# Expert weights in 32 KB homes, a scan of both halves in one tile, and x2 transposes with their squares in PSUM

## The chip, the cores and the metric

The kernel runs on one core of a Trainium2 chip. The core has a matrix engine (PE), a vector engine (DVE), a scalar engine (ACT), GpSimd (POOL) and the SP queue, which issues all loads and stores here; the data moves on 16 DMA engines. The metric is the time of one execution on the device in microseconds, as a median of several runs.

## What is computed

One layer of a decoder for 256 tokens of width 2048, in float32. The first half is a block of two mixers; the second is a mixture of 32 experts, of which each token uses two.

```python
h = rms_norm(x, attn_norm_g)
u_ssm, q, k, v, gate_ssm, gate_att = jnp.split(h @ w_in, splits, axis=-1)
y_ssm = s5_mixer(u_ssm, ...)      # 64 groups, 64 complex states each:
                                  # s[t] = abar * s[t-1] + bbar u[t];  y = Re(C s) + d u
                                  # z = gelu(y); y_ssm = z * sigmoid(z @ w_glu)
y_att = stick_breaking_attention(rms_norm(q), rms_norm(k), v)    # 8 heads of 128
merged = sigmoid(gate_ssm) * (y_ssm @ w_branch_ssm) + sigmoid(gate_att) * (y_att @ w_branch_att)
x = x + merged @ w_out
h2 = rms_norm(x, ffn_norm_g)
# router: top 1 of 4 groups, then top 2 of the 8 experts in it -> combine[t, e]
for e in range(32):               # w_gate, w_up: 2048 x 512; w_down: 512 x 2048
    hid = silu(h2 @ w_gate[e]) * (h2 @ w_up[e])
    out = out + combine[:, e:e + 1] * (hid @ w_down[e])
x = x + out
```

## The kernel before

**Dense stage.** All dense weights are streamed in 200 steps of 512 KB. In each step SP loads a tile `raw` five steps ahead (`dma`, L129), ACT casts it to `wh`, DVE makes the remainder `wl = raw - wh` two steps ahead (`split`), and PE runs 12 matmuls of 128x512. `raw`, `wh` and `wl` have three buffers each. The matrices follow each other as u, qkv, gates, branch weights `wba`, `wglu` (steps 144 to 151), `wbs` (152 to 167) and `wout` (168 to 199). Between the steps a planner runs generators for the small work: `init_stats`, `attention` with `heads`, `ssm`, `scan` and `gelu`. Each is resumed while the estimated loads of PE, DVE and ACT (the class `Meter`, through which every operation of the three engines goes, so that they all have line L77 in the profile) stay within a bound of one another; a negative yield makes a generator rest for some steps.

**Scan.** The states of the mixer lie in two tiles `Vs`, one for each half of the groups, [128, 2, 16, 128]. `scan` (L502 to L521) walks over the 127 last columns: for each column and half one product `prod` of 128x64 and two additions of 128x32, as soon as that half is ready. Then `ssm` makes `y` out of it block by block with matmuls against `CBD`.

**Residual and router.** After `wout`, `x2_tr(n, t)` (L380 to L394) transposes a quarter of row block t of `x2` into a PSUM tile `ps` (`bga`), ACT copies it out to `xt2`, and the sum of squares is taken by ACT (n < 3) or DVE (n = 3) with the squares themselves written to a spare tile `junk`. At the end of the dense stage DVE reduces the sums (`r2`), and a chain of small operations makes the router's choice. `gather(q)` then fetches the tokens of four experts into `XB`.

**Experts.** `gate_up` (L1109) uses four pieces of weights (k4 = 0 to 3, 32 matmuls of 128x256 each), `down` (L1137) two; after every fourth expert `scatter` adds the results. A piece is 2 MiB, [128, 4, 1024] float32, 16 KB for each partition, and in memory, too, each partition's 16 KB lie in one run. The pieces go through a ring of eleven 16 KB slots: eight units `U` that the dense stage has stopped using, and three slots that come when its pools are closed; from piece 22 on, ten slots. `load_piece` (L867 to L886) issues one load as soon as the next slot has been used. The first seven pieces are loaded under the dense stage as 28 single loads of 512 KB (L881), one in every second step from step 136 on, which stand in the list `ahead` and go out after the step's `raw` (L953); the eighth goes out near step 196. All loads stand in the one SP queue. At the end, `gate_up` of experts 30 and 31 runs `keep_busy(24)`, 24 transposes of a constant, ahead of each piece, and the down pieces come last, in the order 30, 31, 30, 31; the very last is loaded in two halves of 1 MiB.

Of the kernel before, what the change touches and what calls it, by code (L numbers as in the profile page):

```python
# [17 lines left out]
P = 128  # L18
T = 256
# [63 lines left out]
def hybrid_block(ctx, tc, A, out):  # L83
# [7 lines left out]
    U = {i: ctx.enter_context(tc.tile_pool(name=f"u{i}", bufs=1)) for i in range(11) if i != 6}  # L91

    def unit(i, shape, dt, name):
        return U[i].tile(shape, dt, name=name, tag="u")

    def slot(h, shape, dt, name):
        return hp.tile(shape, dt, name=name, tag=f"h{h}")
# [5 lines left out]
    hp = wctx.enter_context(tc.tile_pool(name="hp", bufs=1))  # L103
# [57 lines left out]
    uge = cq.tile([P, P], F32, name="uge")  # L161
# [5 lines left out]
    nmask = cq.tile([P, P], F32, name="nmask")  # L167
# [149 lines left out]
    def glu_fin(n):  # L317
        def f(a):
            if n == 0:
                ys = unit(7, [P, 2, 8, T], F32R, "ys")  # L320
# [59 lines left out]
    def x2_tr(n, t):  # L380
        ps = bg_tile(0)
        for i in range(4):
            k = 4 * n + i
            pe.transpose(ps[:, P * i:P * i + P], S["x2"][:, t, P * k:P * k + P], ident)
        xt = S["xt2"][n, t] = slot((2 * n + t) % 4, [P, 4, P], F32, "xt2")
        act.copy(xt, ps.rearrange("p (i c) -> p i c", i=4))
        junk = slot(4 + (2 * n + t) % 4, [P, 512], F32, "junk")
        xs = S["x2"][:, t, 512 * n:512 * n + 512]
        if n < 3:
            act.activation(junk, xs, AF.Square, accum_out=ssq[:, t, n:n + 1])  # L390
# [70 lines left out]
    xsq01 = slot(0, [P, 2, T], F32, "xsq01")  # L461
    xsq = [xsq01[:, 0], xsq01[:, 1], slot(1, [P, T], F32, "xsq2")]
# [36 lines left out]
    coef = [cq.tile([P, 2, 2, 16], F32, name=f"coef{h}") for h in range(2)]  # L499
    prod = [cq.tile([P, 2, 2, 16], F32, name=f"prod{h}") for h in range(2)]  # L500

    def scan(Vs):  # L502
        at = [1, 1]
        while ("V", 0) not in prog:
            yield 0
        yield -1
        while min(at) < P:
            on = [h for h in range(2) if ("V", h) in prog and at[h] < P]
            for h in on:
                X, c = Vs[h], at[h]  # L510
                vec.tensor_tensor(prod[h], X[:, :, :, c - 1][:, :, None, :].to_broadcast([P, 2, 2, 16]), coef[h], op=OP.mult)
            for k in range(2):
                for h in on:
                    X, c = Vs[h], at[h]
                    vec.tensor_tensor(X[:, :, :, c], X[:, :, :, c], prod[h][:, k], op=OP.add)
            for h in on:
                at[h] += 1
            if len(on) == 1:
                load["vec"] += 0.4
            yield 1 if on else 0  # L520
        prog["scan"] = True  # L521

    def ssm():
# [72 lines left out]
        for h in range(2):  # L596
            hs = slice(16 * h, 16 * h + 16)
            SE.tensor_copy(coef[h][:, 0, 0], a2r[:, hs])
            SE.tensor_copy(coef[h][:, 0, 1], a2i[:, hs])
            SE.tensor_scalar(coef[h][:, 1, 0], a2i[:, hs], -1.0, None, op0=OP.mult)  # L600
            SE.tensor_copy(coef[h][:, 1, 1], a2r[:, hs])
# [74 lines left out]
        CB = cq.tile([P, 16, 32], F32, name="CB")  # L676
# [17 lines left out]
        Vs = [unit(7 + h, [P, 2, 16, P], F32, f"Vs{h}") for h in range(2)]  # L694
        gens.append(scan(Vs))
        gens.append(gelu())
        for b in range(8):
            tiles = [bg_tile(0), bg_tile(1)]
            for ri in range(2):
                for i in range(2):  # L700
                    r = slice(64 * i, 64 * i + 64)
                    for a in range(2):
                        pe.matmul(tiles[i][:, T * a + P * ri:T * a + P * ri + P], BT[r, 2 * b + a, ri], uS[r, 2 * b + a],
                                  start=True, stop=True, tile_position=(64 * i, 0))
            for i in range(2):
                src = tiles[i].rearrange("p (a r c) -> p r a c", a=2, r=2)
                j = 4 * (b % 4) + i
                act.copy(Vs[b // 4][:, :, j:j + 3:2], src)
            if b % 4 == 3:
                prog["V", b // 4] = True  # L710
            yield 0
# [3 lines left out]
        for b in range(8):  # L715
            pp = [bg_tile(0), bg_tile(0)]
            X = Vs[b // 4]
            for par in (1, 0):
                ps = pp[par]
                for si in range(3):  # L720
                    for j in range(4):
# [6 lines left out]
                        elif par == 1:  # L728
                            pe.matmul(ps[js, 0:P], CBD[:, si - 1, 4 * b + j], X[:, si - 1, i],
                                      start=False, stop=(si == 2), tile_position=(0, 32 * j))  # L730
                        else:
                            pe.matmul(ps[js, 1:P], CBD[:, 1 + si, 4 * b + j], X[:, si - 1, i, 0:P - 1],
# [5 lines left out]
    def gelu():  # L738
# [4 lines left out]
        zz = unit(9, [P, 2, 8, T], F32R, "zz")  # L743
# [28 lines left out]
    def attention():  # L772
# [20 lines left out]
        QT = [slot(h, [P, 2, T], F32, f"qkT{h}") for h in range(8)]  # L793
# [11 lines left out]
        AT = unit(4, [P, 2, 2, 2, 3, P], F32, "AT")  # L805
        gens.insert(0, heads(QT, AT[:, 0], (0, 2)))
        gens.insert(1, heads(QT, AT[:, 1], (4, 6)))

    def heads(QT, at, firsts):
# [4 lines left out]
        for h0 in firsts:  # L814
# [32 lines left out]
            for i in range(2):  # L847
                y = slot(h0 + i, [P, 2, T], F32R, f"ya{h0 + i}")
# [7 lines left out]

    ring = [U[i] for i in (10, 8, 9, 2, 7, 4, 3, 1)]
    used = [0]
    held = {}
    ahead = []  # L860
    pieces = [(e, i) for e in range(NE - 2) for i in range(6)]
    pieces += [(e, i) for e in (NE - 2, NE - 1) for i in range(4)]
    pieces += [(e, i) for i in (4, 5) for e in (NE - 2, NE - 1)]
    ptile = {}
    nextp = [0]

    def load_piece():  # L867
        n = nextp[0]
        if n >= len(pieces):
            return  # L870
        j = n % 11 if n < 22 else (n - 22) % 10
        j += n >= 22 and j > 5
        if used[0] <= held.get(j, -1):
            return
        held[j] = n
        e, i = pieces[n]
        tl = ring[j].tile([P, 4, 1024], F32, name="ew", tag="u")
        src = A["wgu"][e][:, 4 * i:4 * i + 4] if i < 4 else A["wd"][e][:, 4 * i - 16:4 * i - 12]
        if n < 7:
            for k in range(4):  # L880
                ahead.append(lambda k=k: sp.dma_start(tl[:, k], src[:, k]))  # L881
        else:
            for c0, cw in (((0, 1024),) if n < len(pieces) - 1 else ((0, LSPLIT), (LSPLIT, 1024 - LSPLIT))):
                sp.dma_start(tl[:, :, c0:c0 + cw], src[:, :, c0:c0 + cw])
        ptile[e, i] = tl
        nextp[0] += 1  # L886

# [29 lines left out]
    first_out = nsub - 32  # L917
    for i in range(nsub):
# [28 lines left out]
        if i == first_out - X2_AT:  # L947
# [5 lines left out]
        if i >= first_out - X2_AT - 8 and (i % 2 == 0 or 0 <= i - first_out + X2_AT < 4):  # L953
            if not ahead and nextp[0] < 7:
                load_piece()
            if ahead:
                ahead.pop(0)()
        if i == nsub - 4:
            load_piece()
    while pend:  # L960
        prog["step"] += 1
        run_pend()
# [3 lines left out]
    for i in range(3):  # L966
        ring.append(ctx.enter_context(tc.tile_pool(name=f"w{i}", bufs=1, reuse_waits="tile")))
# [93 lines left out]

    XY = unit(0, [P, 2, 16, P], F32, "XY")
# [46 lines left out]
    def gate_up(e, gen):  # L1109
        q, i = divmod(e, 4)  # L1110
        gu = acc_tile()
        for k4 in range(4):
# [5 lines left out]
            w = ptile[e, k4]  # L1118
            for kk in range(4):
                k = 4 * k4 + kk  # L1120
                for j in range(4):
                    pe.matmul(gu[32 * j:32 * j + 32, 0:T], XB[:, k, 32 * i:32 * i + 32], w[:, kk, T * j:T * j + T],
                              start=(k == 0), stop=(k == 15), tile_position=(0, 32 * j))
            used[0] += 1
            load_piece()
# [11 lines left out]
    def down(e, hT, dn, c0, cw):  # L1137
        i = e % 4
        w = ptile[e, 4 + c0 // 1024]
        n4 = cw // 4  # L1140
        for j in range(4):
            for c in range(4):
                x0 = c0 % 1024 + n4 * c
                pe.matmul(dn[32 * c:32 * c + 32, c0 // 4:c0 // 4 + n4], hT[:, 32 * j:32 * j + 32],
                          w[:, j, x0:x0 + n4], start=(j == 0), stop=(j == 3), tile_position=(0, 32 * c))
        if (c0 + cw) % 1024 == 0:
            used[0] += 1
            load_piece()
# [3 lines left out]
    def scatter(q, n, ts=(0, 1)):  # L1152
        if q == 0 and n == 0:
            S["acc"] = unit(3, [P, 2, D], F32, "accv")
# [9 lines left out]
    while nextp[0] < 11:  # L1164
        load_piece()
# [27 lines left out]
    XO = unit(2, [P, 16, T], F32, "XO")  # L1193
    WO = [unit(u, [P, 4, 1024], F32, f"WO{u}") for u in (4, 9, 7, 0)]
    hO = unit(8, [P, 2, 512], F32, "hO")
    hOT = unit(1, [P, 4, T], F32, "hOT")
# [94 lines left out]
```

## Time and profile before

| | us |
|---|---|
| median of 3 runs | 1557.23 |
| lowest, highest | 1555.97, 1557.52 |
| profiled execution, its own time | 1555.73 |
| its span in the trace | 1553.9 |
| PE, DVE, ACT, POOL busy | 1252.9, 540.5, 451.1, 48.1 |
| DMA, all bytes | 516.91 MB, 333 GB/s over the span |

A busy time counts instructions from start to end, whether the engine works at full clock or not, so a share over the whole span mixes stages with different limits. The span falls into a dense stage (to 626 us), a hand-over with the router (to about 660 us), the experts, and a tail of some 35 us; each has to be read by itself. The times of the text are microseconds from the start of the span. Idle time of an engine counts only where another waits for it.

### The profile page before, as it was taken

To read this page: it belongs to the slowest core of one execution; us is meant where nothing else is said; L and a number is where in the kernel's file an instruction comes from. 1 tells how busy PE (TensorE), PEld (TensorE's weight loads), DVE (VectorE), ACT (ScalarE), POOL (GpSimd) and SP (SyncE) were. 2 spreads that over 40 slices of the span, in tenths; PEclk is the share of its full clock that TensorE was granted. 3 is DMA by queue.
4 is the path that set the end of the run, shared out by engine and by line. 5 is a ranking of instruction groups with operands and counts; after the bars stand their busy time and mean duration, and the time that the engine had idled before them with its cause. 6 is when DMAs were issued, how large, how long until landed. Compare 5 with 4: busy or idle time off the path is not lost. (4 is left out here: it accounts for less than half of the span.)

```text
span 1553.9 us, 25147 instructions
## 1 busy us (share of the span) xinstructions
PE 1252.9 (81%) x10662; PEld 856.7 (55%) x10662; DVE 540.5 (35%) x1344; ACT 451.1 (29%) x768; POOL 48.1 (3%) x105
## 2 busy tenths in 40 slices
PE   9999999999999999878558558557657657656697
PEld 8888888888878888644224224224223324323364
DVE  6746788898866744302002002002002002002001
ACT  5654577544454444121101100110110110110101
POOL 6500000000000000000000000000000000000000
PEclk9999999999999999999789779888888889879899
DMA  7645555566658877999999999999999999999996
GB/s 259 200 148 161 178 163 162 162 191 191 190 189 287 273 270 245 382 427 428 427 426 428 426 427 427 427 427 428 426 428 427 427 427 427 427 427 427 427 427 259
DMA packets 65108, 516.91 MB, mean 333 GB/s; under 512 B 7905, under 2 KB 8161, under 8 KB 41441
## 3 DMA queue, kind: packets, MB, share of 16 engines
q1 hardware_dynamic: 64704, 515.21, 84.4%
q8 instruction: 86, 1.41, 0.4%
q14 instruction: 30, 0.24, 0.0%
q10 hardware_dynamic: 288, 0.06, 0.0%
HBM read 513.14 MB, written 2.10 MB: 332 GB/s over the span
## 5 line engine op out<-in xcount | busy, mean ns | idle before, releaser
L77 PE MATMUL acc<-ew,XY 128*32 128x256 f32 x4096 | 309.1, 455 | 169.9 <-DMA ew<-wgu 169.8
L77 PEld LDWEIGHTS acc<-ew,XY 128*32 128x32 f32 x4096 | 142.3, 126 | 320.7 <-DMA ew<-wgu 189.1
L77 DVE TENSOR_TENSOR wl<-raw,wh 128x1024 fp32r<-128x1024 f32 (+1 forms) x201 | 244.1, 1217 | 140.6 <-ACT wh L77 139.3
L77 ACT CAST wh<-raw 128x1024 fp32r<-128x1024 f32 x199 | 208.6, 1053 | 179.0 <-PE acc L77 113.7
L77 DVE TENSOR_TENSOR sg<-sg,acc 128x128 f32<-128x128 f32 x32 | 9.2, 288 | 660.2 <-ACT sg L77 660.2
L77 PE MATMUL acc<-ew,hT 128*32 128x256 f32 (+1 forms) x2080 | 149.2, 436 | 71.3 <-DMA ew<-wd 39.4
L77 ACT COPY XY<-acc 32x256 f32<-32x256 f32 (+1 forms) x260 | 93.7, 360 | 209.8 <-PE acc L77 207.3
L77 PEld LDWEIGHTS acc<-ew,hT 128*32 128x32 f32 x2080 | 73.6, 123 | 138.3 <-issue 54.8
L77 PE MATMUL acc<-wh,xh 128*128 128x512 f32 x512 | 144.8, 399 | 1.1 <-DVE wh L77 0.8
L77 PE MATMUL acc<-wh,xl 128*128 128x512 f32 x512 | 140.3, 391 | 0.0
L77 PE MATMUL acc<-wl,xh 128*128 128x512 f32 x512 | 140.0, 390 | 0.0
L77 ACT ACTIVATE sg<-acc 128x128 f32<-128x128 f32 x32 | 8.9, 278 | 416.0 <-PE acc L77 416.0
L77 PEld LDWEIGHTS acc<-wh,xl 128*128 128x128 f32 x512 | 96.6, 189 | 20.6
L77 PEld LDWEIGHTS acc<-wl,xh 128*128 128x128 f32 x512 | 96.5, 189 | 20.3
L77 PEld LDWEIGHTS acc<-wh,xh 128*128 128x128 f32 x512 | 93.4, 189 | 20.2 <-issue 1.2
L77 DVE TENSOR_TENSOR Vs<-Vs,prod 128x32 f32<-128x32 f32 x508 | 76.9, 222 | 0.0
L77 PE MATMUL acc<-XY,sc 128*128 128x512 f32 x128 | 61.9, 624 | 14.7 <-ACT XY L77 14.5
L77 PE MATMUL bga<-SL,x 128*128 128x128 f32 x512 | 63.5, 280 | 10.3 <-DVE SL L77 10.3
L77 PEld LDWEIGHTS bga<-SL,x 128*128 128x128 f32 x512 | 59.0, 192 | 22.9 <-DVE SL L77 15.9
L77 DVE TENSOR_TENSOR accv<-accv,acc 128x512 f32<-128x512 f32 x56 | 38.5, 688 | 79.9 <-PE acc L77 79.9
L77 PE MATMUL acc<-wh,m 128*128 128x512 f32 x256 | 64.6, 392 | 0.0
L77 DVE TENSOR_TENSOR prod<-Vs,coef 128x64 f32<-128x64 f32 x254 | 56.1, 263 | 0.0
(222 smaller groups left out, 972.5 us busy)
## 6 DMA issues: line engine op xcount, KB each, us to landing
ew<-wgu SPq DMA_DIRECT2D x123, 2048.0 KB, 39.3
ew<-wd SPq DMA_DIRECT2D x61, 2048.0 KB, 39.4
raw<-win SPq DMA_DIRECT2D x127, 512.0 KB, 4.2
raw<-wout SPq DMA_DIRECT2D x32, 512.0 KB, 4.2
ew<-wgu SPq DMA_DIRECT2D x20, 512.0 KB, 5.6
raw<-wba SPq DMA_DIRECT2D x16, 512.0 KB, 4.5
raw<-wbs SPq DMA_DIRECT2D x16, 512.0 KB, 4.8
raw<-wglu SPq DMA_DIRECT2D x8, 512.0 KB, 5.5
```

The costliest lines, as they stand in the source:

```text
L77: return f(out, *args, **kw)
```

## The change

- **Homes.** The units are put together in homes: A, B and C of 32 KB for each partition (two old units each), the single units Z, V, S, T and X of 16 KB, and W of 32 KB where the three late slots were. Several tensors of the dense stage move to other units (`ys`, `ya`, `zz`, `qt`), and the pool of spare slots `hp` is gone.
- **Expert loads.** In the first round, up to (2,16-24), loads are of 2 MiB (4 rows of 4 KB for each partition) or, under the dense stage, single rows; from the third expert on they are of 4 MiB, 32 KB in one run for each partition, in turn to W, A, B, C. 44 rows of 512 KB fit in the first round, 32 after it. Under the dense stage 32 single rows are loaded instead of 28, in two of three steps from step 150 on; `x2` is loaded in steps 145 to 149. `used(e, r)` gives back row by row, and at each fourth row issues whatever loads fit.
- **Last experts.** The four down loads keep their sizes and order; the gate_up loads of experts 30 and 31 are of 4 MiB like the others. The fillers stay.
- **Scan.** Both halves stand in one tile; the scan begins when both are ready, and each column takes one product of 128x128 and two additions of 128x64. The planner is told 0.5 us more for each column than before.
- **x2 transposes.** The squares go into `ps` instead of `junk`.

```diff
     def scan(X):
+        while ("V", 1) not in prog:
             yield 0
         yield -1
...
+        for c in range(1, P):
+            vec.tensor_tensor(prod, X[:, :, :, c - 1][:, :, None, :].to_broadcast([P, 2, 2, 32]), coef, op=OP.mult)
             for k in range(2):
+                vec.tensor_tensor(X[:, :, :, c], X[:, :, :, c], prod[:, k], op=OP.add)
+            load["vec"] += 0.5
+            yield 1
...
         act.copy(xt, ps.rearrange("p (i c) -> p i c", i=4))
-        junk = slot(4 + (2 * n + t) % 4, [P, 512], F32, "junk")
...
-            vec.scalar_tensor_tensor(junk, xs, 1.0, xs, op0=OP.mult, op1=OP.mult, accum_out=ssq[:, t, n:n + 1])
+            vec.scalar_tensor_tensor(ps, xs, 1.0, xs, op0=OP.mult, op1=OP.mult, accum_out=ssq[:, t, n:n + 1])
...
+    pieces = [(0, 0, 8, "A", 0), (0, 8, 16, "B", 0), (0, 16, 20, "S", 0), (0, 20, 24, "T", 0), (1, 0, 8, "C", 0),
+              (1, 8, 12, "V", 0), (1, 12, 16, "W", 0), (1, 16, 20, "W", 4), (1, 20, 24, "A", 0), (2, 0, 4, "A", 4),
+              (2, 4, 8, "B", 0), (2, 8, 12, "B", 4), (2, 12, 16, "S", 0), (2, 16, 24, "C", 0)]
+    first = len(pieces)
+    for e in range(3, NE):
+        for r in range(0, 16, 8):
+            pieces.append((e, r, r + 8))
+        if e < NE - 2:
+            pieces.append((e, 16, 24))
+    pieces += [(NE - 2, 16, 24), (NE - 1, 16, 24)]
+    pieces = [p if n < first else (*p, "WABC"[(n - first) % 4], 0) for n, p in enumerate(pieces)]
...
+    def used(e, r):
+        for k in [k for k, v in holds.items() if v == (e, r)]:
+            del holds[k]
+        if r % 4 == 3:
+            while load_piece():
+                pass
...
-        if i >= first_out - X2_AT - 8 and (i % 2 == 0 or 0 <= i - first_out + X2_AT < 4):
-            if not ahead and nextp[0] < 7:
-                load_piece()
-            if ahead:
-                ahead.pop(0)()
-        if i == nsub - 4:
+        if not ahead and nextp[0] < EARLY and i >= READY[nextp[0]] and (i != nsub - 1 or nextp[0] < EARLY - 1):
             load_piece()
+        if ahead and (i % 3 or i >= nsub - 4):
+            ahead.pop(0)()
```

A piece (e, lo, hi, home, at) is rows lo to hi of expert e: rows 0 to 15 are gate and up, 16 to 23 down.

**SP queue, end of the dense stage and the first round.** `raw` are the loads of the dense stage, `ew` those of expert weights (L881 and L895 single rows, L884 and L897 the rest). Before:

```order
L129 DMA raw<-wout 128x1024 x2
L881 DMA ew<-wgu 128x1024
L129 DMA raw<-wout 128x1024 x2
L881 DMA ew<-wgu 128x1024
L884 DMA ew<-wgu 128x4096 x3
L884 DMA ew<-wd 128x4096 x2
L884 DMA ew<-wgu 128x4096 x4
L884 DMA ew<-wd 128x4096 x2
```

and now:

```order
L141 DMA raw<-wout 128x1024
L895 DMA ewC<-wgu 128x1024
L141 DMA raw<-wout 128x1024 x2
L895 DMA ewC<-wgu 128x1024
L141 DMA raw<-wout 128x1024
L895 DMA ewC<-wgu 128x1024 x3
L897 DMA ewV<-wgu 128x4096
L897 DMA ewW<-wgu 128x4096
L897 DMA ewW<-wd 128x4096
...
L897 DMA ewC<-wd 128x8192
L897 DMA ewW<-wgu 128x8192
```

The single rows stand closer together, and the loads after the first round have twice the length.

**SP queue, the last loads.** Before, with experts 30 and 31 as the last rows of `wgu`:

```order
L884 DMA ew<-wgu 128x4096 x8
L884 DMA ew<-wd 128x4096 x3
L884 DMA ew<-wd 128x4x512 x2
L1162 DMA out<-accv 128x512 x8
```

and now:

```order
L897 DMA ewA<-wgu 128x8192
L897 DMA ewB<-wgu 128x8192
L897 DMA ewC<-wgu 128x8192
L897 DMA ewW<-wgu 128x8192
L900 DMA ewA<-wd 128x4096
L900 DMA ewB<-wd 128x4096
L903 DMA ewA<-wd 128x4096
L905 DMA ewB<-wd 128x4x512 x2
L1189 DMA out<-accv 128x512 x8
```

Eight gate_up loads have become four; the down loads and the stores are the same.

**DVE, end of the dense stage.** The squares of the last quarter of `x2`, for the two row blocks, and the reduce that opens the router; the numbers in the names are those of the tiles. Before:

```order
L77 SCALAR_TENSOR_TENSOR junk_5926,ssq_159<-x2_4618 128x512 [waits DVE_49]
L77 SCALAR_TENSOR_TENSOR junk_5935,ssq_159<-x2_4618 128x512 [waits DVE_49]
L77 TENSOR_REDUCE r2_5997<-ssq_159 128x2 [waits DVE_49]
```

and now:

```order
L77 SCALAR_TENSOR_TENSOR bga_5490,ssq_150<-x2_4188 128x512 [waits DVE_49,Activation_49]
L77 SCALAR_TENSOR_TENSOR bga_5498,ssq_150<-x2_4188 128x512 [waits DVE_49,Activation_49]
L77 TENSOR_REDUCE r2_5559<-ssq_150 128x2 [waits DVE_49]
```

Each of the two squares has a wait for ACT in addition, whose copy reads the same PSUM tile `bga`.

## Rows read from the trace of the kernel before

**Rows 1.** The page: bandwidth of the DMA engines in 40 equal slices

```profile
GB/s 259 200 148 161 178 163 162 162 191 191 190 189 287 273 270 245 382 427 428 427 426 428 426 427 427 427 427 428 426 428 427 427 427 427 427 427 427 427 427 259
```

**Rows 2.** Stretches: us; PE, PEld, DVE, ACT, POOL busy; clock, DMA share, GB/s

```profile
0.00:626.00 626.00, 623.21 (x3477) 517.84 (x3478) 446.42 (x1133) 332.68 (x429) 48.06 (x105) 1.00 0.64 206
...
636.00:640.00 4.00, 4.00 (x51) 2.95 (x51) 0.85 (x2) 0.00 (x0) 0.00 (x0) 1.00 0.76 324
640.00:644.00 4.00, 4.00 (x43) 3.68 (x46) 1.20 (x2) 0.00 (x0) 0.00 (x0) 1.00 0.86 299
...
700.00:1520.00 820.00, 547.17 (x6097) 287.42 (x6090) 74.03 (x140) 96.36 (x279) 0.00 (x0) 0.86 1.01 427
...
1430.00:1440.00 10.00, 9.06 (x108) 7.38 (x112) 3.12 (x7) 0.00 (x0) 0.00 (x0) 1.00 1.02 434
...
1466.00:1480.00 14.00, 9.98 (x97) 3.92 (x85) 0.29 (x1) 0.54 (x2) 0.00 (x0) 0.51 1.00 426
```

**Rows 3.** Waits of PE from 0 to 626 us, longest first: sum, times, longest

```profile
PE acc L77 <- POOL ident masks.py:199: 1.4, 1, 1.4
```

**Rows 4.** Waits of PE from 700 to 1520 us for loads

```profile
PE acc L77 <- DMA ew<-wgu: 165.5, 77, 3.4
```

**Rows 5.** The page, groups: count, busy us and mean ns, idle time before

```profile
L77 DVE TENSOR_TENSOR Vs<-Vs,prod 128x32 f32<-128x32 f32 x508 | 76.9, 222 | 0.0
```

**Rows 6.** Waits of ACT from 480 to 620 us for loads

```profile
ACT wh L77 <- DMA raw<-wbs: 4.7, 2, 2.4
...
ACT wh L77 <- DMA raw<-wout: 1.8, 1, 1.8
```

**Rows 7.** Timeline of DVE and ACT at 627 us: start, us

```profile
627.71 0.69 DVE L77 SCALAR_TENSOR_TENSOR junk<-x 128x512 f32<-128x512 f32 x1
...
628.44 0.16 DVE L77 TENSOR_REDUCE r<-ssq 128x2 f32<-128x8 f32 x1
...
627.93 0.59 ACT L77 COPY xt<-bga 128x512 f32<-128x512 f32 x1 [0.41 <-PE bga L77]
```

**Rows 8.** Timeline of PE: the first expert piece

```profile
637.75 1.93 PE L77 MATMUL acc<-ew,XY 128*32 128x256 f32 x32
```

**Rows 9.** The last three loads, as issued (start, us) and to landing (KB, us)

```profile
1495.91 0.33 SPq L884 DMA_DIRECT2D ew<-wd  x1
...
1500.80 0.39 SPq L884 DMA_DIRECT2D ew<-wd  x1
...
1505.64 7.34 SPq L884 DMA_DIRECT2D ew<-wd  x1
...
ew<-wd SPq DMA_DIRECT2D x1, 2048.0 KB, 39.4
...
ew<-wd SPq DMA_DIRECT2D x1, 1024.0 KB, 37.2
...
ew<-wd SPq DMA_DIRECT2D x1, 1024.0 KB, 34.9
```

**Rows 10.** The load of the last gate_up piece: issue (start, us), then to landing

```profile
1481.24 0.33 SPq L884 DMA_DIRECT2D ew<-wgu  x1
...
ew<-wgu SPq DMA_DIRECT2D x1, 2048.0 KB, 39.1
```

**Rows 11.** Timeline of PE in the last 90 us

```profile
1471.58 3.64 PE L77 MATMUL acc<-ew,XY 128*32 128x256 f32 x32 [2.89 <-DMA ew<-wgu]
...
1515.58 1.93 PE L77 MATMUL acc<-ew,XY 128*32 128x256 f32 x32
1517.45 2.84 PE L77 MATMUL acc<-ident 128*128 128x128 f32 x24
1520.35 1.93 PE L77 MATMUL acc<-ew,XY 128*32 128x256 f32 x32
...
1543.94 3.23 PE L77 MATMUL acc<-XY,sc 128*128 128x512 f32 x6
```

**Rows 12.** Waits of PE from 1500 to 1554 us, longest first

```profile
PE acc L77 <- ACT XY L77: 2.6, 2, 1.8
...
PE acc L77 <- DMA ew<-wgu: 0.2, 1, 0.2
```

More of the change, by code (lines that the diff above doesn't have):

```diff
@@ L496, in init_stats, with scan @@
         yield 0.8
[L499 to L504, printed above, removed]
+    coef = shaped(k2[:, 256:384], [P, 2, 2, 32])
+    prod = shaped(k2[:, 384:512], [P, 2, 2, 32])
+    def scan(X):
+        while ("V", 1) not in prog:
             yield 0
         yield -1
[L507 to L511, printed above, removed]
-            for k in range(2):
[L513 to L520, printed above, removed]
+        for c in range(1, P):
+            vec.tensor_tensor(prod, X[:, :, :, c - 1][:, :, None, :].to_broadcast([P, 2, 2, 32]), coef, op=OP.mult)
+            for k in range(2):
+                vec.tensor_tensor(X[:, :, :, c], X[:, :, :, c], prod[:, k], op=OP.add)
+            load["vec"] += 0.5
+            yield 1
         prog["scan"] = True
@@ L792, in attention @@
         yield 0
-        QT = [slot(h, [P, 2, T], F32, f"qkT{h}") for h in range(8)]
+        QT = [qt[:, h] for h in range(8)]
         for h in range(8):
@@ L854, in heads @@
             prog["att"] = True
[L857 to L865, printed above, removed]
+    EARLY = 6
+    pieces = [(0, 0, 8, "A", 0), (0, 8, 16, "B", 0), (0, 16, 20, "S", 0), (0, 20, 24, "T", 0), (1, 0, 8, "C", 0),
+              (1, 8, 12, "V", 0), (1, 12, 16, "W", 0), (1, 16, 20, "W", 4), (1, 20, 24, "A", 0), (2, 0, 4, "A", 4),
+              (2, 4, 8, "B", 0), (2, 8, 12, "B", 4), (2, 12, 16, "S", 0), (2, 16, 24, "C", 0)]
@@ new lines, in hybrid_block, with source @@
+    first = len(pieces)
[6 more added lines that the diff above has]
+    pieces = [p if n < first else (*p, "WABC"[(n - first) % 4], 0) for n, p in enumerate(pieces)]
+    last = len(pieces) - 1
+    holds, room, where, ahead, nextp = {}, {}, {}, [], [0]
+    def source(e, lo, hi):
+        return A["wgu"][e][:, lo:hi] if hi <= 16 else A["wd"][e][:, lo - 16:hi - 16]
@@ L885, in load_piece @@
-        ptile[e, i] = tl
-        nextp[0] += 1
+        if n > last:
+            return False
+        e, lo, hi, h, at = pieces[n]
+        if any((h, at + r) in holds for r in range(hi - lo)):
+            return False
+        if h not in room:
+            room[h] = H[h].tile([P, 4 if h in "STV" else 8, 1024], F32, name="ew" + h, tag="u")
+        tl = room[h][:, at:at + hi - lo]
+        for r in range(lo, hi):
+            where[e, r] = room[h][:, at + r - lo]
+            holds[h, at + r - lo] = e, r
@@ L965, in hybrid_block @@
     rt = ctx.enter_context(tc.tile_pool(name="rt", bufs=1, reuse_waits="tile"))
-    for i in range(3):
-        ring.append(ctx.enter_context(tc.tile_pool(name=f"w{i}", bufs=1, reuse_waits="tile")))
+    H["W"] = ctx.enter_context(tc.tile_pool(name="homeW", bufs=1, reuse_waits="tile"))
     def keep_busy(n):
@@ L1138, in down @@
         i = e % 4
-        w = ptile[e, 4 + c0 // 1024]
+        w = [where[e, 16 + 4 * (c0 // 1024) + j] for j in range(4)]
         n4 = cw // 4
```

125 lines of the change are left out of this document (68 added, 57 removed).

## The prediction

> **What bounds the kernel now.** I read the bandwidth line of the page first, because it shows the stages: 148 to 287 GB/s in the first sixteen slices, 382 in the next, then 426 to 428 GB/s in every slice but the last [rows 1]. So the kernel has two limits, and each edit is priced in the stage in which it stands. The busy times by stretch say which limit rules where. From 0 to 626 us PE is busy for 623.2 of 626.0 us at a granted clock of 1.00 (2.4 GHz) while the DMA engines are used at 0.64; from 700 to 1520 us the DMA share is 1.01 at 427 GB/s while PE is busy for 547 of 820 us [rows 2]. The waits agree: in the dense stage PE's longest is 1.4 us, for POOL right at the start [rows 3]; in the expert stage it waits 77 times for an expert tile, 165.5 us in all [rows 4]. Two short stretches belong to neither. At the hand-over the DMA share falls to 0.76 and 0.86 [rows 2], with the ring full and the next load waiting for PE to free a slot; and in the last 35 us PE runs through a fixed row of fillers and weight pieces.
>
> **Dense stage: 0.** The scan loses half of its instructions: 508 additions (76.9 us of DVE) become 254 of twice the width [rows 5], and 254 products become 127. All of it is DVE time under a PE that waits for nobody, so it buys nothing. The y matmuls, now one block per step over eight steps instead of eight blocks in one, are the same matmuls; PE's sum is unchanged. What could cost something is the SP queue: 32 single 512 KB expert loads, in two of three steps, where there were 28 in every second step. They stand between the `raw` loads that feed the split. In 480 to 620 us ACT, which makes `wh`, waits for such loads only 4.7 us in two places and 1.8 us in one [rows 6], and PE waits for none of it [rows 3]; the load per step rises from one raw and a half single to one raw and two thirds, at a DMA share that leaves room [rows 2]. I take 0; if the raws come late it is a rival below.
>
> **Router: +0.8 us.** The squares of the last quarter of x2 now go into the PSUM tile that ACT is copying out, so DVE has to wait for both copies. Before, the second square starts at 627.71, takes 0.69, and the reduce that opens the router follows at 628.44; ACT's second copy starts at 627.93 and takes 0.59, ending at 628.52 [rows 7]. After: 628.52 + 0.69 + 0.04 of issue = 629.25, against 628.44. Behind the reduce lies the whole router chain, then the gather, then the first expert piece on PE, which starts at 637.75 and frees the first slot at 639.68 [rows 8]. Nothing else is late there, so the first slot comes free 0.8 us later, and with it everything that the DMA queue does afterwards. Bounds 0 to 1.0.
>
> **Four more early rows: 0, first-round depth +0.3.** Two more MiB are loaded under the dense stage, worth 4.9 us of transfer at 427 GB/s. But the first round holds 22 MiB before and after (eleven slots of 2 MiB; 44 rows of 512 KB), and the queue already runs dry at the hand-over: 0.24 of 4 us and 0.14 of 4 us idle [rows 2]. Bytes that arrive earlier only lengthen this idle time; the next load still needs PE's first release. The slots come free in the same 2 MiB steps in the first round. At its end (2,16-24) and the first rotating pieces need 4 MiB free before anything is issued, so the queue is shallower for one or two pieces; between 0 and the 1.5 us that was idle at the hand-over, I take 0.3.
>
> **Steady stage: -5.5 us.** From the third expert on, 2 MiB loads (128 rows of 16 KB) become 4 MiB loads (128 rows of 32 KB), 86 of them. Nothing else bounds that stage, so only the rate matters, and no row shows a 32 KB run. The nearest rows are the last three weight loads: 2 MiB in 16 KB runs, then two of 1 MiB in 2 KB runs. They land at 1495.91 + 39.4 = 1535.3, 1500.80 + 37.2 = 1538.0 and 1505.64 + 34.9 = 1540.5 [rows 9], that is 2.6 us per MiB in 2 KB runs. A MiB in 16 KB runs is 2.46 us at 427 GB/s. The 0.16 us belong to 512 runs instead of 64, per engine 32 instead of 4, so one run costs some 5.7 ns more than its bytes (an estimate). A 4 MiB load now has 8 instead of 16 runs on each of 16 engines: 8 x 5.7 = 46 ns, times 84 loads that are in the 427 GB/s stretch is 3.9 us. The lower bound is 0: a run may be cut at 16 KB inside, or the rate may be set by something that does not count runs. The upper bound is the fastest stretch there is: 434 GB/s over 10 us [rows 2], 1.6 per cent of 820 us, 13 us. I take 5.5, near the worked value and on the side of the upper one, because that difference of 0.16 comes from landings given to a tenth.
>
> The page DMA: Bandwidth & Descriptors of the Trainium skill (Why small descriptors are slow) puts the fixed price at about 3 cycles for each packet, one cycle carrying 32 bytes. By that 16 KB runs lose 0.6 and 32 KB runs 0.3 per cent, an estimate of 2.4 us where I take 5.5, and the total would be 3 us later. The same page, under Where 436 GB/s comes from, gives a ceiling of 435 GB/s, which bears on the upper bound; the 434 GB/s row agrees with it.
>
> **Tail: +5.6 us.** Before, each 2 MiB piece of the last two experts is followed on PE by 24 fillers, 2.84 us, and 32 matmuls, 1.93 us: 4.77 us, just under the 4.9 us between landings. The last gate_up piece is issued at 1481.24 and lands 39.1 us later, at 1520.3 [rows 10]; its matmuls start at 1520.35 [rows 11]. After, (31,8-16) is one load of 4 MiB, so its first half, too, can't start before 1520.3: first half 1.93, fillers 2.84, second half 1.93. The second half starts at 1525.1, 4.77 us later. Behind it stand silu, the transpose, the two down pieces, the scatter and the stores, all in PE's order with fillers between, and there PE's longest waits are for ACT, 2.6 us in all, and only 0.2 us for a load [rows 12]: the later steps have no slack that would take the shift up, and their weights, loaded in the same order and sizes as before, are there already. So the last matmuls move from 1543.94 [rows 11] by the full 4.77. To this comes the clock: before, PE runs its piece at 1471.58 in 3.64 us instead of 1.93 [rows 11], at a granted clock of 0.51 (1.2 GHz) from 1466 to 1480 [rows 2], after waiting for loads. Waits of 4 MiB are longer, so the two halves of the last ordinary down may run at that level and gate_up of expert 30 may begin late: 0 to 2.6 us, taken 0.8.
>
> **Sum.** The profiled execution took 1555.73 us, 1.5 less than the median 1557.23. 0.8 + 0.3 + 5.6 - 5.5 = 1.2: 1556.9 in such an execution, 1558.4 as a median, given as 1558.5.
>
> **Rivals.**
> *A 32 KB run is no faster.* Against the sum only the rate term is gone, and the 4 MiB wait in the tail decides: 1557.2 + 0.8 + 0.3 + 5.6 = 1564. For it: 427 GB/s is held so evenly over 22 slices [rows 1] that it looks like a ceiling. Against it: the 434 GB/s stretch and the slower 2 KB runs. It decides, and the kernel is slower by more than 0.2 per cent (3.1 us, about what a measurement of this kernel can tell from no change), when the rate gives less than 3.6 us.
> *The rate gains much.* If the whole distance to 434 GB/s is overhead of runs, 10 to 13 us come off against 6.7 us of costs: 1551 to 1554. For it: the estimate per run is coarse, and half as many completions have to be handled. Against: 2 KB runs, eight times as many, cost only 6 per cent.
> *The early rows pay.* If the hand-over isn't limited by free slots, 4.9 us come off: 1553.6. Against: the DMA share of 0.76 there [rows 2].
> *Raws late.* If the denser singles hold up `raw` loads beyond ACT's and DVE's lead, each of the some 30 steps with a single could lose up to 0.4 us: 1562 to 1570. For it: three waits of ACT for raws already there [rows 6].
> The page named above also has a rule (Anatomy of one DMA) of 2.0 us for each DMA beside its bytes, by which some 85 fewer loads would save 170 us. Loads that follow each other every 4.9 us with none of it visible speak against it, chance under 1 in 100.
>
> **How the numbers follow.** Forecast 0.46 (1555.5 to 1561), no faster run 0.26, large gain 0.18, early rows 0.04, late raws 0.06. Faster takes the large gain, the early rows and a small part of the forecast: 0.24. Slower takes the first rival, late raws, and nothing else: 0.32, less what of the first rival stays near the bound, 0.30. The rest, 0.46, is within 0.2 per cent. The range runs from 1550.5 (gain of 13, the tail as forecast) to 1565.5 (no gain, all costs but the highest clock loss).
>
> **What would show it.** Right: the expert stage at about 430 GB/s; the last 64 gate_up matmuls of expert 31 in two groups of 1.93 us that start only when their load lands, and some 38 us instead of 33.5 from there to the end; the reduce 0.8 us later than its squares were; no new PE wait before 626 us. Wrong: the expert stage still at 427 GB/s or at 434; a tail as short as before, which would mean that some step behind it had slack; a hand-over in which the DMA share rises; raw waits of PE.

## Result and profile after

| | before | after |
|---|---|---|
| median, us | 1556.69 (4 runs) | 1575.87 (4 runs, 1573.9 to 1578.36) |
| profiled execution, us | 1555.73 | 1578.36 |
| its span, us | 1553.9 | 1576.6 |

The change makes the kernel slower: ratio 1.0122, 95% interval 1.011 to 1.0135, some 19 us. The forecast was 1558.5 with a range up to 1565.5, so the time lies outside it. The traced execution of the changed kernel is the slowest of its four and that of the kernel before lies below the median, so sums taken from the two traces come out larger than 19 us.

The page of the changed kernel: busy times (us, share of the span, instructions), then bandwidth in 40 slices and packets.

```profile
PE 1263.1 (80%) x10662; PEld 870.3 (55%) x10662; DVE 541.3 (34%) x963; ACT 451.8 (29%) x768; POOL 45.3 (3%) x101
...
GB/s 264 184 146 154 187 136 156 164 187 211 189 108 190 315 296 299 293 406 431 431 430 429 433 427 435 426 433 429 431 432 430 428 433 427 431 431 428 424 426 205
DMA packets 53150, 516.86 MB, mean 328 GB/s; under 512 B 6576, under 2 KB 6832, under 8 KB 40624
```

Against [rows 1] the expert stage has risen from 427 to about 430 GB/s. Yet the stage in which nothing should have happened has changed: the twelfth slice (434 to 473 us) falls to 108 GB/s, and the slope to 430 comes later. PE's waits from 0 to 626 us, longest first (us in all, times, longest):

```profile
PE acc L77 <- ACT zz L77: 10.0, 1, 10.0
PE acc L77 <- ACT wh L77: 4.1, 4, 1.5
PE acc L77 <- POOL ident masks.py:199: 1.4, 1, 1.4
```

The last of them is the row that stood first before [rows 3]. Of the two above it the first is new, and the second was 0.2 us in all before. The first expert piece shows the whole loss. Timeline of PE (start, us, and in brackets the idle time before it and what ended it):

```profile
477.92 3.84 PE L77 MATMUL acc<-zz,wh 128*128 128x256 f32 x16 [10.04 <-ACT zz L77]
481.55 1.77 PE L77 MATMUL acc<-zz,wl 128*128 128x256 f32 x8
...
659.32 1.93 PE L77 MATMUL acc<-ewA,XY 128*32 128x256 f32 x32
```

The expert piece starts at 659.32 instead of 637.75 [rows 8], 21.6 us later, while the span has grown by 22.7. From there to the end the kernel takes 917.3 us, before 916.2. So the stages from the first expert piece on come out at +1.1, and the dense stage, put at 0, holds nearly everything.

Where in the dense stage, by the starts of the same matmuls in both timelines:

| first matmul of | before | after | later by |
|---|---|---|---|
| step 20 | 66.92 | 69.25 | 2.3 |
| step 100 | 324.89 | 331.28 | 6.4 |
| step 132 | 411.93 | 418.32 | 6.4 |
| step 144 (`acc<-zz,wh`) | 459.54 | 477.92 | 18.4 |
| step 152 (after `wglu`) | 483.80 | 504.47 | 20.7 |
| step 196 | 615.41 | 636.08 | 20.7 |

14.3 us arise between step 132 and step 152, around the hand-over from the scan to `wglu`; 6.4 before: 2.3 by step 20, and 4.1 more by step 100.

### The profile page after: what moved, and what is told of

The parts are those of the page before. It is cut to its first block, busy times and chain, and to the rows that moved or that the text cites. A ratio compares the mean times of both kernels' runs of the same rounds, so it can differ in the third digit from the quotient of the medians.

```text
span 1576.6 us, 24577 instructions
## 1 busy us (share of the span) xinstructions
PE 1263.1 (80%) x10662; PEld 870.3 (55%) x10662; DVE 541.3 (34%) x963; ACT 451.8 (29%) x768; POOL 45.3 (3%) x101
## 5 line engine op out<-in xcount | busy, mean ns | idle before, releaser
L77 PE MATMUL acc<-ewA,XY 128*32 128x256 f32 x992 | 81.1, 496 | 53.4 <-DMA ewA<-wgu 53.4
L77 PE MATMUL acc<-ewC,XY 128*32 128x256 f32 x1024 | 76.4, 457 | 37.4 <-DMA ewC<-wgu 37.4
L77 PE MATMUL acc<-ewB,XY 128*32 128x256 f32 x1024 | 72.1, 442 | 29.8 <-DMA ewB<-wgu 29.5
L77 PEld LDWEIGHTS acc<-ewA,XY 128*32 128x32 f32 x992 | 40.9, 141 | 92.7 <-issue 42.8
L77 PE MATMUL acc<-XY,sc 128*128 128x512 f32 x128 | 68.6, 681 | 14.7 <-ACT XY L77 14.5
L77 PEld LDWEIGHTS acc<-ewC,XY 128*32 128x32 f32 x1024 | 35.8, 131 | 72.1 <-DMA ewC<-wgu 40.7
L77 DVE TENSOR_TENSOR homeA<-homeA,k 128x64 f32<-128x64 f32 x254 | 72.2, 284 | 8.8
L77 PE MATMUL acc<-ewW,XY 128*32 128x256 f32 x992 | 63.5, 405 | 14.5 <-DMA ewW<-wgu 14.5
```

The source lines that it names most:

```text
L77: return f(out, *args, **kw)
```

## What happens between steps 132 and 152

The timelines of PE, ACT and DVE of the changed kernel before and in the wait:

```profile
458.18 0.42 PE L77 MATMUL bga<-homeB,CB 32*32 32x128 f32 x8
...
462.99 0.42 PE L77 MATMUL bga<-homeB,CB 32*32 32x128 f32 x8
...
465.13 1.05 ACT L77 CAST wh<-raw 128x1024 fp32r<-128x1024 f32 x1
...
468.50 2.17 ACT L77 ACTIVATE homeB<-homeB 128x512 f32<-128x512 f32 x4
...
473.50 2.44 ACT L77 ACTIVATE homeB<-homeB 128x512 f32<-128x512 f32 x4 [1.89 <-DVE homeB L77]
477.25 2.42 ACT L77 CAST zz<-homeB 128x512 fp32r<-128x512 f32 x4 [1.31 <-DVE homeB L77]
...
461.41 1.23 DVE L77 TENSOR_TENSOR wl<-raw,wh 128x1024 fp32r<-128x1024 f32 x1 [3.59 <-ACT wh L77]
...
472.78 2.49 DVE L77 SCALAR_TENSOR_TENSOR homeB<-homeB 128x512 f32<-128x512 f32 x4
475.19 1.42 DVE L77 TENSOR_SCALAR homeB<-homeB 128x512 f32<-128x512 f32 x4
476.53 2.49 DVE L77 SCALAR_TENSOR_TENSOR homeB<-homeB 128x512 f32<-128x512 f32 x4
```

This is gelu, all four block pairs of it, between y (`homeB`) and `wglu` (which reads `zz`). It begins at 468.5, after the last y block (its matmuls are `bga<-homeB,CB` and `bga<-homeA,CBD`, and the last block begins at 462.99), and PE has nothing left but `wglu`, which needs it. In the eight steps before, where the y blocks now run one by one, 4.81 us apart, DVE did nothing but one `wl` per step and was idle for 3.59 us of each 4.81. So gelu could have run there, and did not.

The code says why. The planner asks the generators in the order of a list, `ssm` (which makes y) ahead of `gelu`, and stops asking in a step once PE's estimated load has grown by more than `BURST` = 1.0. By the estimate of `Meter` a y block adds 1.3 us to it; in the trace a y block lengthens its step by 2.1. Thus in each of the eight steps y runs and gelu is passed over. In the kernel before, the scan ended so late that no y block had been made when step 144 asked for `zz`; there the generators are run in turn without that bound, and gelu's stages went in between the y blocks. The kernel before, from its first y block to the first matmul of `wglu` (y is in `uy` there):

```profile
444.66 0.42 PE L77 MATMUL bga<-uy,CB 32*32 32x128 f32 x8
...
448.90 0.63 ACT L77 ACTIVATE uy<-uy 128x512 f32<-128x512 f32 x1
...
449.57 0.69 DVE L77 SCALAR_TENSOR_TENSOR uy<-uy 128x512 f32<-128x512 f32 x1 [1.92 <-ACT uy L77]
...
454.30 0.62 ACT L77 CAST zz<-uy 128x512 fp32r<-128x512 f32 x1
...
459.54 2.18 PE L77 MATMUL acc<-zz,wh 128*128 128x256 f32 x16
```

The y blocks in one piece were the cover of gelu. The wide scan, done by step 135, took the cover away. After the wait PE also runs slower for a while: the first 24 matmuls of `wglu` take 3.84 and 1.77 us, and the granted clock between 478 and 482 us, third from the end in the columns of [rows 2], is 0.50 (1.2 GHz):

```profile
478.00:482.00 4.00, 4.00 (x19) 4.00 (x20) 3.43 (x6) 1.88 (x4) 0.00 (x0) 0.50 0.02 4
```

## Experiments

Two theories for the dense loss. **A (lost cover):** as just told. **B (homes):** the new places of the tensors (`zz` after `qt`, y and its copies in home B) make gelu or `zz` wait. A was tried from two sides. Beside the experiments the kernel before took 1557.7 to 1557.8 us, 1 us more than in the table above, so medians of different sets compare to about 1 us.

### The scan a little slower

```diff
-            load["vec"] += 0.5
+            load["vec"] += 0.6
```

> The changed kernel with one number altered: the scan tells the planner 0.6 us more per column instead of 0.5, so that the scan ends some nine steps later and the eight y blocks come in one piece at the start of step 144, as in the kernel before. Theory A (lost cover): with 0.5 the scan is done by step 135, one y block per step takes 2.1 us of PE, over the planner's bound of 1.0, and gelu is passed over in each of these steps; at step 144 PE then waits 10.0 us for zz, restarts at a lower clock (2.3 us) and has spent 1.9 us more on the spread y blocks. With 0.6 all of this goes: 14 us less, 1575.9 to some 1562, no wait of PE for zz over 1 us. Theory B (homes): zz and gelu come late because their tiles now share a home with others (zz after qt in S); then the wait for zz stays and the time stays within 3 us of 1575.9.

Measured: 1560.75 us median (1557.55 to 1562.06), 15.1 less than the changed kernel. PE's waits up to 626 us hold no `zz` any more; PE and then ACT at step 144:

```profile
461.50 0.64 PE L77 MATMUL bga<-homeA,CBD 128*32 128x127 f32 x16
462.08 2.17 PE L77 MATMUL acc<-zz,wh 128*128 128x256 f32 x16
...
456.04 0.27 ACT L77 COPY homeB<-bga 128x128 f32<-128x128 f32 x1
456.67 0.28 ACT L77 COPY homeB<-bga 128x128 f32<-128x128 f32 x1 [0.36 <-PE bga L77]
456.83 0.62 ACT L77 CAST zz<-homeB 128x512 fp32r<-128x512 f32 x1
```

The first part of `zz` is made at 456.83, between two copies of y blocks, and the first matmul on `zz` follows the last y block at once. The homes are the same, so B falls. The matmuls on `zz` run at once in 2.17 us, not 3.84: the lower clock after 10 us of idle PE was part of the price. By the starts of the same matmuls, steps 132 to 152 take what they took in the kernel before, so all 14.3 us are back. The altered number does one thing more: steps 64 to 100, which had lost 4.1 us in the changed kernel, lose 1.5 here.

### gelu asked first

```diff
-        gens.append(gelu())
+        gens.insert(0, gelu())
```

> The changed kernel with the gelu generator put ahead of the others in the planner's list, so that it is asked before the y block of the step; scan and y blocks stay where they are (steps 136 to 143). Theory A: gelu's stages for the first blocks now run beside the later y blocks, and only the chain of the last block pair is left for step 144: the wait for zz falls from 10.0 to 4 to 5 us and the clock falls for a shorter time, 5 to 8 us less in all, 1568 to 1571. Theory B (homes): no change, 1575.9 within 3 us. A third, that the spread y blocks alone cost the time by their PE work: no change in the time either, but the wait for zz gone.

Measured: 1564.63 us (1563.56 to 1565.83), 11.2 less than the changed kernel, more than expected. The y blocks stay at one per step, but in 440 to 470 us DVE is busy for 12.91 us where it was for 7.36 (changed kernel first, then this one; the columns are those of [rows 2]):

```profile
440.00:470.00 30.00, 27.87 (x336) 18.69 (x328) 7.36 (x6) 11.70 (x23) 0.00 (x0) 1.00 0.38 114
```

```profile
440.00:470.00 30.00, 29.57 (x334) 20.93 (x335) 12.91 (x17) 15.31 (x28) 0.00 (x0) 1.00 0.38 113
```

The wait for `zz` is gone altogether. I had thought that the last pair's chain would still be exposed for 4 to 5 us; but the first `wglu` matmuls need only the first pairs, and the last is finished beside them. By the starts of the matmuls, steps 132 to 152 still cost 2.3 us more than before. Most of that is the y blocks: one by one they lengthen their eight steps from 2.72 to 4.81 us, 16.7 us in all, while in one piece, in the run above, they take from 447.19 to 462.08, 14.9 us. The rest of what stays against the run above, some 4 us by the medians, lies in steps 64 to 100, which lose 4.1 us here as in the changed kernel.

### The tail: gate_up loads of experts 30 and 31 in 2 MiB

```diff
-            sp.dma_start(tl, source(e, lo, hi))
+            for r in (range(lo, hi, 4) if e >= NE - 2 else (lo,)):
+                m = 4 if e >= NE - 2 else hi - lo
+                sp.dma_start(tl[:, r - lo:r - lo + m], source(e, r, r + m))
```

> The changed kernel with the gate_up loads of experts 30 and 31 as eight loads of 2 MiB instead of four of 4 MiB, in the same homes, all else the same. Theory of the prediction: the last gate_up piece's first half no longer waits for the second, 4.6 to 4.8 us less, 1575.9 to some 1571, and from the landing of the last gate_up load to the end 33.5 us instead of 38.4. Rival (slack behind it): the time stays within 1.5 us, and the stretch from landing to end stays at 38.

Measured: 1576.09 us (1575.43 to 1578.37): no change that can be told from none. The tail of the changed kernel on PE:

```profile
1499.38 3.64 PE L77 MATMUL acc<-ewW,hT 128*32 128x256 f32 x32 [4.02 <-DMA ewW<-wd]
...
1504.63 1.93 PE L77 MATMUL acc<-ewW,hT 128*32 128x256 f32 x32 [1.60 <-ACT XY L77]
...
1509.26 1.93 PE L77 MATMUL acc<-ewA,XY 128*32 128x256 f32 x32
...
1533.54 1.93 PE L77 MATMUL acc<-ewC,XY 128*32 128x256 f32 x32
...
1538.18 1.93 PE L77 MATMUL acc<-ewW,XY 128*32 128x256 f32 x32
1540.04 2.84 PE L77 MATMUL acc<-ident 128*128 128x128 f32 x24
1542.81 1.93 PE L77 MATMUL acc<-ewW,XY 128*32 128x256 f32 x32
...
1566.32 3.23 PE L77 MATMUL acc<-XY,sc 128*128 128x512 f32 x6
```

Its last gate_up load, issued at 1506.62 (KB, us to landing):

```profile
ewW<-wgu SPq DMA_DIRECT2D x1, 4096.0 KB, 31.5
```

The load lands at 1506.62 + 31.5 = 1538.1, its first half starts at 1538.18 and its second 4.63 us later: what the prediction had said. But the pieces of the row follow each other every 4.63 us, so PE, which began the piece before at 1533.54, would have come to this one at 1538.17 in any case. And the same places with the loads split:

```profile
1501.27 1.93 PE L77 MATMUL acc<-ewW,hT 128*32 128x256 f32 x32 [1.60 <-ACT XY L77]
...
1505.91 1.93 PE L77 MATMUL acc<-ewA,XY 128*32 128x256 f32 x32
...
1539.26 1.93 PE L77 MATMUL acc<-ewW,XY 128*32 128x256 f32 x32
...
1562.77 3.23 PE L77 MATMUL acc<-XY,sc 128*128 128x512 f32 x6
```

and the last gate_up load, issued at 1503.27:

```profile
ewW<-wgu SPq DMA_DIRECT2D x1, 2048.0 KB, 33.5
```

Now the last piece lands at 1536.8 but starts only at 1539.26. From the end of down(29) on, PE goes through its row of fillers and pieces nearly without a gap, 4.63 us each, so the row cannot follow the loads more closely than it has begun. From its first piece to the last block of matmuls it takes 57.1 us in the changed kernel and 56.9 here, and 57.4 before, where that piece started so:

```profile
1486.50 1.93 PE L77 MATMUL acc<-ew,XY 128*32 128x256 f32 x32
```

And the row begins late, since down(29) is itself fed by a 4 MiB load: in the changed kernel its first half waits 4.02 us for the whole load and then runs in 3.64 us instead of 1.93. From the landing of the last gate_up piece to the last block of matmuls it was 1543.94 - 1520.3 = 23.6 us before [rows 10, 11], 28.2 in the changed kernel, 26.0 here. In this trace the first half of down(29) ran in 1.93 us, at full clock, so 1.7 of the 2.2 us between the last two need not come from the split.

### The tail from down(29) on

On the kernel with 0.6, loads of 2 MiB from the down load of expert 29 on.

```diff
+            m = 4 if (e, lo) >= (NE - 3, 16) else hi - lo
+            for r in range(lo, hi, m):
+                sp.dma_start(tl[:, r - lo:r - lo + m], source(e, r, r + m))
```

> The run with 0.6 per column, and in addition the down load of expert 29 and the gate_up loads of experts 30 and 31 as 2 MiB loads. The run that split only the gate_up loads had moved the time by less than 1.5 us, since PE began the row of fillers late, after the second half of down(29). Theory (the row of fillers is PE-bound, 4.63 us per piece, and what counts is when down(29) lets it start): from the landing of the last gate_up load to the end some 35 us instead of 38.8, and 4 us less in all, 1560.75 to some 1557. Rival (the split of the gate_up loads was all that there was to gain): 1 to 2 us less, 1559 to 1560.

Measured: 1555.91 us (1553.33 to 1557.38), 4.8 less than with 0.6 alone; against the kernel before 0.9985 (0.9976 to 0.9994). PE at the end of down(29) and at the last block:

```profile
1480.85 1.93 PE L77 MATMUL acc<-ewW,hT 128*32 128x256 f32 x32 [1.61 <-ACT XY L77]
...
1485.49 1.93 PE L77 MATMUL acc<-ewA,XY 128*32 128x256 f32 x32
...
1543.32 3.23 PE L77 MATMUL acc<-XY,sc 128*128 128x512 f32 x6
```

The last gate_up load:

```profile
ewW<-wgu SPq DMA_DIRECT2D x1, 2048.0 KB, 36.9
```

Issued at 1482.85, it lands at 1519.75; the stretch from there to the last block is 23.6 us, as before the change. The row itself takes 57.8 us; neither half of down(29) waits for its load any more or runs at the lower clock, where with 0.6 alone they took 3.64 and 3.27 us. The tail's price was where the filler row begins, not at its last piece.

### Two smaller repairs

The squares of the last quarter into a PSUM tile of their own:

```diff
+        sq = acc_tile("sq") if n == 3 else ps
...
-            vec.scalar_tensor_tensor(ps, xs, 1.0, xs, ...)
+            vec.scalar_tensor_tensor(sq, xs, 1.0, xs, ...)
```

> The run before it, and in addition the squares of the last quarter of x2 go into a PSUM tile of their own, so that DVE no longer waits for ACT's copies. Theory: the reduce starts 0.8 us earlier behind the last addition to x2 and the end moves by as much: 0.8 us less than the run before it, some 1556. Rival (the first round of expert loads hides it): the reduce moves, the end does not.

Measured: 1554.03 us (1550.79 to 1558.4). DVE of the changed kernel, then of this one:

```profile
647.16 0.69 DVE L77 TENSOR_TENSOR x<-x,acc 128x512 f32<-128x512 f32 x1 [0.68 <-PE acc L77]
...
649.22 0.70 DVE L77 SCALAR_TENSOR_TENSOR bga<-x 128x512 f32<-128x512 f32 x1 [0.24 <-ACT xt L77]
...
650.01 0.16 DVE L77 TENSOR_REDUCE r<-ssq 128x2 f32<-128x8 f32 x1
```

```profile
627.41 0.69 DVE L77 TENSOR_TENSOR x<-x,acc 128x512 f32<-128x512 f32 x1 [0.68 <-PE acc L77]
...
629.45 0.16 DVE L77 TENSOR_REDUCE r<-ssq 128x2 f32<-128x8 f32 x1
```

From the last addition to the reduce it is 2.85 us with the wait for ACT and 2.04 without. The first expert piece is 0.9 us later than the dense stage alone explains in the changed kernel, and 0.1 here, so the repair reaches PE's first piece. That the end moved by this 0.8 us fits the medians, 1.9 apart, but the runs of both scatter by 4 us or more, so the time alone does not show it.

Then fillers ahead of expert 29, 12 per piece:

> The run before it, and in addition 12 fillers ahead of each gate_up and down piece of expert 29. Theory: the last pieces before the row of fillers ran at the lower clock (3.42 us instead of 1.93 in the run with 2 MiB loads throughout); with fillers PE is at full clock there and the row starts 1 to 1.5 us earlier: some 1555. Rival: the fillers themselves make down(29) late, and the time grows by 1 to 3 us.

Measured: 1553.53 us (1552.52 to 1554.45). In its trace the second half of down(29) takes 1.93 us, at full clock; the median is 0.5 below the run before it, less than expected and within the scatter.

### The scan as it was, in the new homes

```diff
+        at = [1, 1]
...
+            on = [h for h in range(2) if ("V", h) in prog and at[h] < P]
+            for h in on:
+                vec.tensor_tensor(prod[:, :, :, hs[h]], X[:, :, hs[h], c - 1]..., coef[:, :, :, hs[h]], op=OP.mult)
```

> The changed kernel with the scan of the kernel before (two halves, each started when it is ready, 254 products and 508 additions, no 0.5 us per column) in the new homes. Its y blocks come in one piece at step 144. Theory A (only the place of the y blocks counts, the width of the scan's instructions is worth nothing under PE): as the run with 0.6 per column, 1560.75 within 1.5 us. Rival (one wide scan does save time, or the split scan is better paced in steps 60 to 100): 2 to 4 us above, or below, that run.

Measured: 1557.34 us (1554.29 to 1559.24), 18.5 less than the changed kernel and 3.4 less than the wide scan with 0.6: the rival's case, though its trace shows only 1.3 of the 3.4 in the dense stage. So undoing the scan alone takes back the whole loss, and the rest of the change is worth nothing net: 0.9999 (0.999 to 1.0008) of the kernel before. PE waits nowhere between 215 and 335 us in this run, while in the changed kernel it waited 2.7 us for ACT's `wh` there; in steps 64 to 100 the two differ by 4.2 us.

### All repairs, and the price of the 32 KB run

> All repairs together: the scan in two halves as in the kernel before (y blocks in one piece at step 144), loads of 2 MiB from the down load of expert 29 on, the squares in a PSUM tile of their own, 12 fillers ahead of the pieces of expert 29; 32 KB homes and 4 MiB loads up to there stay. The run with all but the scan had 1553.53, and the scan in halves alone was 3.4 us faster than the wide scan with 0.6 per column, of which its trace showed 1.3 in the dense stage. Theory (the terms add): 1550 to 1552. Rival (part of the 3.4 was chance of the expert stage): 1552 to 1554.

Measured: 1552.85 us (1552.51 to 1554.32), 0.9965 (0.9952 to 0.9978) of the kernel before, some 5 us less, and in the range of the rival. Going from the wide to the split scan gave 0.7 us here, not 3.4, and 0.7 is within the scatter.

The same with every load of 2 MiB:

```diff
-            m = 4 if (e, lo) >= (NE - 3, 16) else hi - lo
+            m = 4
```

> The run before it with every 4 MiB load issued as two of 2 MiB in 16 KB runs, so that the length of the runs is the only difference and the tail is the same. Theory of the prediction: 427 instead of 430 GB/s and 4 to 6 us more than the run before it. Rival (the gain in rate is lost again where PE waits for whole 4 MiB): within 1.5 us of it.

Measured: 1557.75 us (1556.35 to 1559.04), 4.9 more. Stretch from 700 to 1520 us, with 32 KB runs and then with 16 KB:

```profile
700.00:1520.00 820.00, 555.91 (x6230) 306.92 (x6234) 74.01 (x140) 96.12 (x279) 0.00 (x0) 0.85 1.00 430
```

```profile
700.00:1520.00 820.00, 560.09 (x6156) 294.82 (x6157) 73.98 (x140) 96.36 (x279) 0.00 (x0) 0.85 1.01 427
```

The gain reaches most of the way to the end. From the first expert piece to the landing of the last gate_up load it is 877.2 us with 32 KB runs and 883.4 with 16 KB, 6.2 apart, and to the end of the kernel 4.5; the rest is lost in the tail, where the stretch from that landing to the last block is 25.5 us with 32 KB runs and 23.6 with 16 KB: in the first of the two PE's row waits for no load any more.

This edit changes two things together, the length of a run and the number of loads. The traces' records of single DMA packets tell them apart. Each load of 2 MiB with 16 KB runs is eight packets of 16 KB on each engine and one of 4 bytes, each of 4 MiB eight of 32 KB and one of 4 bytes. Their medians between 700 and 1450 us are 613 ns for 16 KB, 1215 ns for 32 KB and 9 ns for 4 bytes. So for 4 MiB an engine spends 8 x 11 = 88 ns less on the longer runs, and 9 ns less because there is one load fewer: the length of the run is most of it. The rate shows some 70 ns of this (427 against 430 GB/s). The same pair of rates on the changed kernel, with its other losses:

> The changed kernel with every 4 MiB load issued as two of 2 MiB one after the other (128 runs of 16 KB each) into the same homes at the same moments. Theory that the run length sets the rate: 427 instead of 430 GB/s between 700 and 1520 us, 0.07 us more per 4 MiB, 6 us over 85 loads, against the 4.8 us that the tail gets back as in the run before it: 1575.9 to some 1577, and 6 us above that run. Rival (the rate comes from homes or release steps, not from the run length): 430 GB/s is kept, and the time is that of the run before it, some 1571.

Measured: 1578.24 us (1576.29 to 1579.37), 2.2 above the run with only the gate_up loads of the last two experts split, where 6 were expected, at 427 against 430 GB/s. From the first expert piece to the landing of the last gate_up load it takes 4.7 us more than that run; part of this comes back, because its tail is split from down(29) on as well.

## Why the prediction was wrong

**Dense stage, 0: wrong, +20.7 us, and this is the step that failed.** It counted what the moved y blocks cost PE, "the same matmuls; PE's sum is unchanged", and took the missing waits of PE [rows 3] to mean that what DVE does there "buys nothing" and costs nothing. It never asked what ran beside the y blocks in the kernel before. Their 15 us were where gelu was hidden, and gelu stands between y and the next matmuls. A wait that does not exist in the trace of before says that the cover is there, not that it is not needed. The order of the changed kernel would have shown it: the operations of gelu follow the last y block on ACT and DVE. Of the 20.7 us, 14.3 are this: 10.0 of wait, some 2.3 of matmuls at the lower clock, some 1.9 of y blocks in single steps. Shown by the two runs that brought the cover back in different ways: of the 14.3 us they take back 14.3 and 11.9 by the starts of the matmuls, and 15.1 and 11.2 in all by the medians. The sign "no new PE wait before 626 us" came out wrong with it. The list of rivals had none for it either: each looked at loads.

**The other 6.4 us of the dense stage** are partly explained. 2.3 lie in the first 18 steps; in the ten other runs with the new homes this stretch comes out between -0.3 and +2.1 against the trace of the kernel before, so it varies from run to run, and its cause is open. 4.1 lie in steps 64 to 100, and they belong to the scan and its pace: 4.0 to 4.1 in all four traces with the wide scan at 0.5, 1.1 to 1.5 in the four with 0.6, and none in the three with the scan in halves, all in the same homes. That the wide scan crowds `wh` and `wl` there is argued from PE's new waits of 2.7 us for `wh`, not shown. The prediction put this at nothing with the rest.

**Router, +0.8: right.** From the last addition to the reduce it is 2.85 us, before 628.44 - 626.50 = 1.94 [rows 7]:

```profile
626.50 0.69 DVE L77 TENSOR_TENSOR x<-x,acc 128x512 f32<-128x512 f32 x1 [0.68 <-PE acc L77]
```

The first expert piece is 21.6 late where the dense stage is 20.7 late, 0.9.

**Early rows 0, first round +0.3: right.** With loads of 2 MiB throughout, the way from the first expert piece to the last gate_up landing takes 883.2 us on the changed kernel and 883.4 on the repaired one, against 882.6: +0.6 to +0.8.

**Steady stage, -5.5: right.** The runs measured 4.9 by the medians, and by the landings 4.4 (878.8 us in the changed kernel against 883.2), 4.7 and 6.2, around the 5.5 taken and above the 3.9 worked out from 2 KB runs. That working put a run at 5.7 ns beside its bytes; by the packets it is some 11. The upper bound rested on a row with 434 GB/s in which the DMA share is 1.02, more than the engines' whole time, so the row counts somewhat too much. The rule of 3 cycles per packet in the Trainium skill, DMA: Bandwidth & Descriptors (Why small descriptors are slow), gave an estimate of 2.4 us; here the measurement is about twice that. The ceiling of 435 GB/s on the same page (Where 436 GB/s comes from) agrees with the trace: 430 GB/s over 820 us, and no slice of the page above 435. The rule of 2.0 us for each DMA in the Trainium skill, DMA: Bandwidth & Descriptors (Anatomy of one DMA), is stated there for DMAs that GpSimd issues, and here SP issues them; 85 loads fewer saved 4.9 us, not 170.

**Tail, +5.6: right in size, wrong in place.** Last landing to last block of matmuls grew by 4.6 us. But the cause was said to be the last gate_up piece, with full 4.77 us for its second half (the sum of 2.84 and 1.93; in the row they overlap and come to 4.63). The nearness of 5.6 and 4.6 is in this respect luck. Splitting these loads gave back 2.2 us of the stretch and nothing measurable of the time; only with down(29) split as well was it 23.6 us again. The prediction had the half of it, "gate_up of expert 30 may begin late", priced at 0.8 for the clock (in the changed kernel the first half of down(29) ran in 3.64 us, in the kernel before already in 3.43); what begins late there is a row of fillers that PE itself paces at 4.63 us, so that a delay at its start is carried to the end.

**The sum.** Without the dense term it holds: from the first expert piece on +1.1 us were measured (in the traces +0.6 for the first round, -4.4 for the rate, +4.9 from the last gate_up landing to the end), +0.4 predicted.

## What to carry to other kernels

When an edit makes background work finish sooner, follow its consumer, not its cost: ask what filled the time between the two before, and whether the planner's bounds still let it run there. An engine without waits shows that its cover holds, not that the cover is free to be moved. And where fillers keep an engine busy, the stage is paced by them: find the instruction at which that row starts, since there an earlier start reaches the end.

## Not expected of the hardware

A run of 32 KB instead of 16 KB for each partition still raises the rate, from 427 to 430 GB/s, with loads that were already 2 MiB: a packet of 32 KB takes 1215 ns, two of 16 KB take 1226. And 10 us of idle PE cost another 2.3 us: the first 16 matmuls after it took 3.84 us instead of 2.17, and the next eight 1.77 instead of 1.12, at a granted clock of 0.50.
